# Down phase and S5 parameters: loads placed later; RWKV norm: one Newton chain for two groups; ScalarE: table loaded at the start

## The chip, the cores and the metric

The kernel runs on one core of a Trainium2 chip. The metric is the device time of one execution in microseconds, here the median of three runs. Two kernels are compared by such medians.

## The reference, cut to what matters

One layer of a decoder trunk on 1024 tokens of width 1024, in float32: three mixers (RWKV-7, a complex diagonal state space called S5, gated linear attention), each behind a sigmoid gate, then cross attention to 256 memory tokens, then a gated MLP with a short convolution, then a last RMSNorm.

```python
def rwkv7_mix(...):                       # 8 heads of 64, state S per head
    ...
    _, y = lax.scan(step, S0, seq)
    mean = jnp.mean(y, axis=-1, keepdims=True)
    var = jnp.mean(jnp.square(y - mean), axis=-1, keepdims=True)
    y = ((y - mean) * lax.rsqrt(var + RWKV_GN_EPS)).reshape(B, L, MIX_W) * ln_w + ln_b
    bonus = jnp.sum(r_h * k_h * r_k, axis=-1, keepdims=True) * v_h
    return (y + bonus.reshape(B, L, MIX_W)) * g

def conv_ffn(h, w_up, conv_w, conv_b, w_down):
    u = h @ w_up                          # 1024 x 5632, then a causal conv of width 3
    ...
    return (jax.nn.silu(gate) * val) @ w_down

    # the layer
    h = rms_norm(x, norm_mix)
    x = x + (gated sum of the three mixers) @ w_out
    x = x + cross_attention(rms_norm(x, norm_xattn), mem_n, ...)
    x = x + conv_ffn(rms_norm(x, norm_ffn), ...)
    return rms_norm(x, norm_final)
```

## The kernel before, in words

Every large product is made of three: a float32 operand is split into a high part, cast on ScalarE (ACT), and a low part, the difference, made on VectorE (DVE); high times high, high times low and low times high are added in PSUM (`split`, `mm3`, L111 to L115 and L127 to L132). Weights come by SyncE's DMA queue (SP) into a ring of four `wraw` tiles, are split into `whi` and `wlo`, and go to TensorE (PE). A scheduler writes a fixed instruction order for each engine from the order of the program, from priorities and from when it takes data to be there. An engine runs its list strictly in that order: an instruction that waits holds up all behind it, also on SP and on GpSimd (POOL), which issue the DMAs. SP's DMAs count on eight semaphores in turn, so each also waits until the DMA eight places ahead of it has landed.

**Start** (`start`, L228). SP loads S5's parameters `s5pk` (128x1076, issued in `run`, L1527), then vectors, the transposed memory `memT` and the first weights of the attention keys (`kv_k`). ACT scales `memT` into `mT` (L260); that is its first instruction with a function table. Then come four x tiles (`xt`), whose squares ACT sums (L212), and the weights of the next `kv_k` block.

**RWKV's second part** (`rw2`, L875). For each of 4 head pairs `pr` and 4 groups `g` of four chunks: products `vl`, `w`, `x`, `z`, `qm` (`rw2_prods`; DVE copies `ps_w` into `qw` at L963 before PE can do `z`), then four state steps one after the other (`rw2_steps`; the new state `s` is made half on DVE, half on ACT), then the norm of a group that was done before (`rw2_norm`, L1006): two reductions on DVE with a subtraction between, a square on ACT, `rsqrt_small` (three instructions, then three Newton rounds of three, L188 to L194) on 64x8 values, a scaling (L1021), four transposes, then scale and bias on ACT, plus the bonus (`ybo`, loaded by SP into a single buffer, L1012), times the gate product (`ps_g`), and a store by POOL. Between these, `fill` puts branch products (`ps_fm`) of the other mixers, which need nothing of RWKV.

**MLP and down phase** (`ffn`, `ffn_down` L1379). The MLP's 22 blocks end with `finish`, which writes the activations `c` to DRAM `d_act` by POOL (L1291), four writes a block, the last two adding to what is there; `c` and `u` live in the tiles `x0` to `x7` (even blocks `x0` to `x3`, odd ones `x4` to `x7`). The down product is done as seven products of halves, `a11`, `s1`, `s2`, `s4`, `s3`, `a12`, `a22`, each of 11 units; a unit reads one 128x512 tile of `d_act` (`araw`, L1410, four buffers), splits it, prepares one weight tile and does 12 matmuls. The weight quarters b11, b12, b22, b21 are loaded by SP (L1405) into places that the MLP leaves free. After the first product the residual x comes back from `d_x` into the same tiles `x0` to `x7` (L1472, POOL), and the sums are added to it (L1442). The `a11` units run between the last matmuls of the MLP.

## Time and profile before

| | before |
|---|---|
| median of three runs | 2205.38 us (2204.23 to 2213.23) |
| profiled execution, its own time | 2206.67 us |
| its span in the profile | 2204.9 us |
| PE busy | 2115.6 us, 96% |
| DVE busy | 1437.3 us, 65% |
| ACT busy | 956.8 us, 43% |
| DMA | 287.68 MB, mean 130 GB/s |

PE is busy 96% of the span, so about 89 us are left in which it does nothing; they lie in a few places, which the timeline of PE with its idle times shows one by one. A row of the timeline gives the start, the duration, the engine, line and operation, and in brackets how long the engine was idle before it and what ended that. The profiled execution is 1.29 us above the median of the runs, and 1.77 us of it lie around the span.

### The profile page before, as it was taken

The numbers are of one execution on the slowest core, as the hardware profiler recorded it, in microseconds if no ns is written. First come the engines' busy times: TensorE is split into PE (matmuls) and PEld (weight loads), VectorE is DVE, ScalarE is ACT, GpSimd is POOL, SyncE is SP. The second block draws the span as 40 slices with busy tenths as digits, with TensorE's granted clock in tenths as the row PEclk, the third lists the DMA queues.
The fourth block names the chain that finished last, engine by engine and source line by source line (L and its number), as shares of the span: only waits on it lengthen the run. The fifth ranks groups of instructions, "written<-read, shape, count | busy, mean of one in ns | idle before, by whom it ended". The sixth has DMA issues, their size and how long they took to land.

```text
span 2204.9 us, 29783 instructions
## 1 busy us (share of the span) xinstructions
PE 2115.6 (96%) x10686; PEld 1734.8 (79%) x10686; DVE 1437.3 (65%) x2813; ACT 956.8 (43%) x1692; POOL 201.6 (9%) x302
## 2 busy tenths in 40 slices
PE   7999999999999999999899999999999999988998
PEld 7877779878888887877787788777677777776886
DVE  6883743555657764676776655657677777777756
ACT  6423253554544442232334444555444444453452
POOL 0100000001111131002100000000011111111000
PEclk9999999999999999999999999999999999999999
DMA  8443332112343356565654232233566566597332
GB/s 259 141 115 91 104 107 55 33 55 63 115 129 121 124 187 179 155 169 129 171 183 142 85 103 79 84 119 108 127 157 167 154 127 135 118 280 248 100 95 105
DMA packets 314611, 287.68 MB, mean 130 GB/s; under 512 B 87408, under 2 KB 248864, under 8 KB 314464
## 3 DMA queue, kind: packets, MB, share of 16 engines
q1 hardware_dynamic: 285808, 203.98, 32.2%
q0 software_dynamic: 28656, 81.80, 13.4%
q8 instruction: 84, 1.38, 0.3%
q14 instruction: 63, 0.52, 0.1%
HBM read 191.38 MB, written 94.34 MB: 130 GB/s over the span
## 4 chain that ended last, share of the span: by engine, by line
PE 78%; DVE 8%; DMA 6%; ACT 4%; issue 2%; SPq 0%; DVEq 0%; ACTq 0%; POOLq 0%
PE ps_fm L132 11%; PE ps_fm L130 11%; PE ps_fm L131 11%; PE ps_q L1267 4%; PE ps_q L1268 4%; PE ps_dm L1438 4%; PE ps_q L1269 4%; PE ps_dn L1438 4%; PE ps_tm L130 3%; PE ps_tm L132 3%; PE ps_tm L131 3%; DMA a<-in_ffn_w_down 2%; PE ps_g L834 1%; DMA araw<-d_act 1%; ACT whi L114 1%
## 5 line engine op out<-in xcount | busy, mean ns | idle before, releaser
L115 DVE TENSOR_TENSOR wlo<-wraw,whi 128x512 fp32r<-128x512 f32 x320 | 220.4, 691 | 277.6 <-ACT whi L114 271.0
L114 ACT CAST whi<-wraw 128x512 fp32r<-128x512 f32 x320 | 197.7, 621 | 448.1 <-PE ps_fm L131 285.8
L130 PE MATMUL ps_fm<-hT,whi 128*128 128x512 f32 x800 | 316.9, 396 | 0.0
L132 PE MATMUL ps_fm<-hT,wlo 128*128 128x512 f32 x800 | 316.3, 395 | 0.0
L131 PE MATMUL ps_fm<-hT,whi 128*128 128x512 f32 x800 | 315.5, 394 | 0.0
L132 PEld LDWEIGHTS ps_fm<-hT,wlo 128*128 128x128 f32 x800 | 150.5, 188 | 33.4 <-issue 1.2
L131 PEld LDWEIGHTS ps_fm<-hT,whi 128*128 128x128 f32 x800 | 150.7, 188 | 32.7 <-issue 0.7
L130 PEld LDWEIGHTS ps_fm<-hT,whi 128*128 128x128 f32 x800 | 150.6, 188 | 31.9 <-issue 0.4
L1267 PE MATMUL ps_q<-a,whi 128*128 128x512 f32 x320 | 127.3, 398 | 6.7 <-ACT u L1345 5.2
L1268 PE MATMUL ps_q<-a,whi 128*128 128x512 f32 x320 | 126.1, 394 | 0.0
L1269 PE MATMUL ps_q<-a,wlo 128*128 128x512 f32 x320 | 126.0, 395 | 0.0
L1282 DVE SCALAR_TENSOR_TENSOR c<-u,cvn,c 128x1023 f32<-128x1023 f32 x80 | 102.5, 1284 | 19.3 <-ACT c L1279 18.0
L1438 PE MATMUL ps_dn<-whi,b 128*128 128x512 f32 x312 | 100.0, 399 | 8.5 <-ACT whi L114 8.5
L1291 POOL DMA_DIRECT2D d_act<-c x77 | 65.6, 859 | 406.9 <-DVE c L1286 258.2
L132 PE MATMUL ps_tm<-whi,a 128*128 128x512 f32 x256 | 101.5, 397 | 0.0
L114 ACT CAST whi<-s 128x512 fp32r<-128x512 f32 x80 | 49.6, 620 | 112.2 <-PE ps_q L1268 81.9
L114 ACT CAST b<-araw 128x512 fp32r<-128x512 f32 x72 | 44.7, 620 | 105.5 <-PE ps_dm L1438 37.8
L115 DVE TENSOR_TENSOR b<-araw,b 128x512 fp32r<-128x512 f32 x72 | 49.5, 690 | 60.9 <-ACT b L114 60.1
L1438 PE MATMUL ps_dm<-whi,b 128*128 128x512 f32 x264 | 82.9, 393 | 0.0
L115 DVE TENSOR_TENSOR wlo<-s,whi 128x512 fp32r<-128x512 f32 x80 | 55.0, 688 | 39.3 <-ACT whi L114 37.4
L130 PE MATMUL ps_fm<-a,whi 128*128 128x512 f32 x192 | 78.9, 411 | 1.7 <-ACT whi L114 1.6
L130 PE MATMUL ps_fm<-b,whi 128*128 128x512 f32 x192 | 76.5, 399 | 2.7 <-DVE c L1282 2.3
(537 smaller groups left out, 5066.3 us busy)
## 6 DMA issues: line engine op xcount, KB each, us to landing
wraw<-in_w_in SPq DMA_DIRECT2D x104, 256.0 KB, 3.0
araw<-d_act SPq DMA_DIRECT2D x77, 256.0 KB, 2.7
d_act<-c POOLq DMA_DIRECT2D x22, 768.0 KB, 7.5
d_gate<-gate SPq DMA_DIRECT2D x24, 512.0 KB, 3.0
gsg<-d_gate SPq DMA_DIRECT2D x24, 512.0 KB, 4.6
wraw<-in_ffn_w_up SPq DMA_DIRECT2D x48, 256.0 KB, 3.8
d_act<-c POOLq DMA_DIRECT2D x11, 1024.0 KB, 6.1
d_act<-c POOLq DMA_DIRECT2D x44, 256.0 KB, 5.3
```

What stands on the lines that cost most here:

```text
L114: self.nc.scalar.copy(hi, src)
L115: self.nc.vector.tensor_tensor(lo, src, hi.bitcast(F32), op=ALU.subtract)
L130: nc.tensor.matmul(ps, lh, rh, start=first, stop=False)
L131: nc.tensor.matmul(ps, lh, rl, start=False, stop=False)
L132: nc.tensor.matmul(ps, ll, rh, start=False, stop=last)
L834: nc.tensor.matmul(ps[:, j * 128:j * 128 + 128], BD[i][:, ci, :], AR[:, :, ci * 64:ci * 64 + 64], start=True, stop=True)
L1267: nc.tensor.matmul(ps, hi[:, s], t[0][:], start=first and k == 0, stop=False, skip_group_check=True)
L1268: nc.tensor.matmul(ps, hi[:, s], t[1][:], start=False, stop=False, skip_group_check=True)
L1269: nc.tensor.matmul(ps, lo[:, s], t[0][:], start=False, stop=last and k == 3, skip_group_check=True)
L1282: v.scalar_tensor_tensor(c[:, t:t1], src[:, t - d:t1 - d], cw(2 - d), c[:, t:t1], op0=ALU.mult, op1=ALU.add)
L1291: to = lambda n0, n1, h, **kw: nc.gpsimd.dma_start(st(n0, n1), src[h].to_broadcast([128, n1 - n0, 512]), **kw)
L1438: nc.tensor.matmul(o, a[x][:, s], w[y], start=first and k == 0, stop=last and k == 2, skip_group_check=True)
```

## The change

It has four parts. S5's parameters are loaded after the first four x tiles instead of first of all (`then` in `start`). ACT gets a multiplication of one column, with nothing to wait for but a memset, so that its function table is loaded then. In `rw2_norm` an even group g stops after the sums of squares; the odd group that follows makes one `rsqrt_small` on 64x16 for both and finishes both, one behind the other; `y` has three buffers for it. In `ffn_down` b12 is loaded during `s1` and b22 during `s2` (each was loaded one product earlier), and x comes by SP in halves of 512 columns, four after each of the products a11, s1, s2 and s4, the gains `gf` last; POOL has no loads left there.

```diff
--- before.py
+++ after.py
@@ -225,8 +225,12 @@
             if whole:
                 nc.scalar.mul(whole(k), ps[:, :n], g)
 
-    def start(self, pool):
-
+    def start(self, pool, then):
+
+
+        warm = self.cp.tile([128, 1], F32, name="warm")
+        self.nc.vector.memset(warm[:], 0.0)
+        self.nc.scalar.mul(warm[:], warm[:], 1.0)
         self.hT = self.new_T(pool, "hT")
         with ExitStack() as c2:
             p = self.pool(c2, "nrm")
@@ -270,6 +274,7 @@
                 norm(xs[h * 4:h * 4 + 4], "nmix", lambda k, l: self.hT[k, l][:, h * 512:h * 512 + 512])
             self.kv_k(0, us)
             load_x()
+            then()
             self.kv_k(1)
             self.kv_k(2)
             self.kv_k(3)
@@ -895,7 +900,7 @@
         f3 = lambda ap: ap.rearrange("p (c t) -> p c t", t=64)
         c3 = lambda ap: ap.rearrange("p (c k) -> p c k", c=4)
         n = 0
-        todo, prev = [], []
+        todo, prev, held = [], [], []
 
         def step():
             pr, g, ops = todo.pop(0)
@@ -904,7 +909,7 @@
 
         def norm():
             if len(prev) > 1:
-                self.rw2_norm(p, *prev.pop(0))
+                self.rw2_norm(p, held, *prev.pop(0))
         for hf in range(2):
             for pr in range(4):
                 t = ring[n % 2]
@@ -939,7 +944,7 @@
                     fill()
         step()
         norm()
-        self.rw2_norm(p, *prev.pop(0))
+        self.rw2_norm(p, held, *prev.pop(0))
 
     def rw2_prods(self, p, c0, t, R, c3):
 
@@ -999,36 +1004,45 @@
                 sn = S0[pr, (ci + 1) % 2]
                 v.tensor_scalar(sn[0:64, 0:64], o[64:128, 0:64], self.rw_pc[64:128, pr, 0, ci + 1:ci + 2], None, op0=ALU.mult)
                 nc.scalar.mul(sn[64:128, 64:128], o[64:128, 64:128], self.rw_pc[64:128, pr, 1, ci + 1:ci + 2])
-        y = p.tile([64, 8, 64], F32, tag="ysb", name="ysb", bufs=2)
+        y = p.tile([64, 8, 64], F32, tag="ysb", name="ysb", bufs=3)
         nc.scalar.copy(y[:], ps[0:64, :].rearrange("p (k f) -> p k f", k=8))
         return y
 
-    def rw2_norm(self, p, pr, g, y):
+    def rw2_norm(self, p, held, pr, g, y):
+
 
         nc, v = self.nc, self.nc.vector
-        ts = slice(g * 256, g * 256 + 256)
-        fs = slice(pr * 128, pr * 128 + 128)
-        bo = p.tile([128, 256], F32, tag="ybo", name="ybo", bufs=1)
-        nc.sync.dma_start(bo[:], self.d_bon[fs, ts])
-        m = p.tile([64, 2, 8], F32, tag="ym", name="ym", bufs=2)
         bc = lambda a: a.unsqueeze(2).to_broadcast([64, 8, 64])
-        v.tensor_reduce(m[:, 0], y[:], axis=AX, op=ALU.add)
-        v.scalar_tensor_tensor(y[:], bc(m[:, 0]), -1.0 / 64, y[:], op0=ALU.mult, op1=ALU.add)
+        if g % 2 == 0:
+            held.append(p.tile([64, 2, 16], F32, tag="ym", name="ym", bufs=2))
+        m, q = held[0], slice(g % 2 * 8, g % 2 * 8 + 8)
+        v.tensor_reduce(m[:, 0, q], y[:], axis=AX, op=ALU.add)
+        v.scalar_tensor_tensor(y[:], bc(m[:, 0, q]), -1.0 / 64, y[:], op0=ALU.mult, op1=ALU.add)
         sq = p.tile([64, 8, 64], F32, tag="ysq", name="ysq", bufs=1)
         nc.scalar.activation(sq[:], y[:], AF.Square)
-        v.tensor_reduce(m[:, 1], sq[:], axis=AX, op=ALU.add)
-        rs = self.rsqrt_small(p, m[:, 1], 1 / 64, 64e-5, 2, 8, 64)
-        v.tensor_tensor(y[:], y[:], bc(rs[:]), op=ALU.mult)
-        ps = self.psm.tile([128, 512], F32, tag="m", name="ps_yt")
-        for c in range(4):
-            nc.tensor.transpose(ps[:, c * 64:c * 64 + 64], y[:, 2 * c:2 * c + 2, :].rearrange("p h f -> p (h f)"), self.ident[0:64, 0:64])
-        yf = p.tile([128, 256], F32, tag="yf", name="yf", bufs=2)
-        nc.scalar.activation(yf[:], ps[:, 0:256], AF.Identity, bias=self.v("lnb", pr), scale=self.v("lnw", pr))
-        v.tensor_tensor(yf[:], yf[:], bo[:], op=ALU.add)
-        ps = self.psm.tile([128, 512], F32, tag="m", name="ps_g2")
-        nc.tensor.matmul(ps[:, 0:256], self.rw_gup[:, fs], self.rw_g[:, ts], start=True, stop=True)
-        v.tensor_tensor(yf[:], yf[:], ps[:, 0:256], op=ALU.mult)
-        nc.gpsimd.dma_start(self.yrw[fs, ts], yf[:])
+        v.tensor_reduce(m[:, 1, q], sq[:], axis=AX, op=ALU.add)
+        held.append((g, y))
+        if g % 2 == 0:
+            return
+        held.pop(0)
+        rs = self.rsqrt_small(p, m[:, 1], 1 / 64, 64e-5, 2, 16, 64)
+        fs = slice(pr * 128, pr * 128 + 128)
+        for q in range(2):
+            g, y = held.pop(0)
+            ts = slice(g * 256, g * 256 + 256)
+            bo = p.tile([128, 256], F32, tag="ybo", name="ybo", bufs=1)
+            nc.sync.dma_start(bo[:], self.d_bon[fs, ts])
+            v.tensor_tensor(y[:], y[:], bc(rs[:, q * 8:q * 8 + 8]), op=ALU.mult)
+            ps = self.psm.tile([128, 512], F32, tag="m", name="ps_yt")
+            for c in range(4):
+                nc.tensor.transpose(ps[:, c * 64:c * 64 + 64], y[:, 2 * c:2 * c + 2, :].rearrange("p h f -> p (h f)"), self.ident[0:64, 0:64])
+            yf = p.tile([128, 256], F32, tag="yf", name="yf", bufs=2)
+            nc.scalar.activation(yf[:], ps[:, 0:256], AF.Identity, bias=self.v("lnb", pr), scale=self.v("lnw", pr))
+            v.tensor_tensor(yf[:], yf[:], bo[:], op=ALU.add)
+            ps = self.psm.tile([128, 512], F32, tag="m", name="ps_g2")
+            nc.tensor.matmul(ps[:, 0:256], self.rw_gup[:, fs], self.rw_g[:, ts], start=True, stop=True)
+            v.tensor_tensor(yf[:], yf[:], ps[:, 0:256], op=ALU.mult)
+            nc.gpsimd.dma_start(self.yrw[fs, ts], yf[:])
 
 
     def gate_w(self, i, j):
@@ -1466,22 +1480,30 @@
                     a, w = act(an, b, ring()), weight(wn, b)
                     for i in range(4):
                         mm(o[i], a, w, i, first and b == 0, last and b == NB - 1)
-            product("a11", "b11", bank["A"], True, False, (load_w("b11"), load_w("b12")))
-            for tt in range(8):
-                x[tt] = self.xt(tt, f"x{tt}")
-                nc.gpsimd.dma_start(x[tt][:], self.d_x[tt * 128:tt * 128 + 128, :])
-            for q in range(2):
-                nc.gpsimd.dma_start(gf[q][:], A["norm_final"][q * 512:q * 512 + 512].partition_broadcast(128))
+            product("a11", "b11", bank["A"], True, False, (load_w("b11"),))
+
+            def load_x(t0, q):
+                for tt in range(t0, t0 + 4):
+                    if x[tt] is None:
+                        x[tt] = self.xt(tt, f"x{tt}")
+                    s = slice(q * 512, q * 512 + 512)
+                    nc.sync.dma_start(x[tt][:, s], self.d_x[tt * 128:tt * 128 + 128, s])
+            load_x(0, 0)
             for i in range(4):
                 add(i, 0, bank["A"][i], ALU.add)
             bank["B"] = second()
-            product("s1", "n1", bank["B"], True, False, (load_w("b22"),))
+            product("s1", "n1", bank["B"], True, False, (load_w("b12"),))
+            load_x(4, 1)
             for i in range(4):
                 add(4 + i, 1, bank["B"][i], ALU.subtract)
-            product("s2", "t2", bank["A"], False, False)
+            product("s2", "t2", bank["A"], False, False, (load_w("b22"),))
+            load_x(0, 1)
             for i in range(4):
                 add(i, 1, bank["A"][i], ALU.add)
             product("s4", "b22", bank["B"], False, True, (load_w("b21"),))
+            load_x(4, 0)
+            for q in range(2):
+                nc.sync.dma_start(gf[q][:], A["norm_final"][q * 512:q * 512 + 512].partition_broadcast(128))
             for i in range(4):
                 add(i, 1, bank["B"][i], ALU.add, True)
             product("s3", "t3", bank["A"], False, False)
@@ -1524,8 +1546,7 @@
         self.d_v = self.dr.tile([256, D], F32, name="d_v")
         hT, c1 = self.pool(left, "hT"), ExitStack()
         pk = self.pool(c1, "s5k").tile([128, 1076], F32, name="s5pk")
-        nc.sync.dma_start(pk[:], A["s5_par"])
-        self.start(hT)
+        self.start(hT, lambda: nc.sync.dma_start(pk[:], A["s5_par"]))
         todo = gates[:13]
 
         def fill(n):
```

The order on three engines. **First, SP at the start of the program**; `vc` are vectors, `wraw` weights of the keys. Before:

```order
L1527 DMA s5pk<-in_s_par 128x1076
L96 DMA vc<-in_cols 128x81
L254 DMA memT_131<-in_memT 128x2x256
L123 DMA wraw<-in_xa_wkv 128x4x128
L254 DMA memT_132<-in_memT 128x2x256
L123 DMA wraw<-in_xa_wkv 128x4x128
L254 DMA memT_133<-in_memT 128x2x256
L254 DMA memT_134<-in_memT 128x2x256
L123 DMA wraw<-in_xa_wkv 128x4x128 x2
L236 DMA xt<-in_x 128x1024 x4
L123 DMA wraw<-in_xa_wkv 128x4x128 x4
```

Now:

```order
L96 DMA vc<-in_cols 128x81
L258 DMA memT_133<-in_memT 128x2x256
L123 DMA wraw<-in_xa_wkv 128x4x128
L258 DMA memT_134<-in_memT 128x2x256
L123 DMA wraw<-in_xa_wkv 128x4x128
L258 DMA memT_135<-in_memT 128x2x256
L258 DMA memT_136<-in_memT 128x2x256
L123 DMA wraw<-in_xa_wkv 128x4x128 x2
L240 DMA xt<-in_x 128x1024 x4
L1549 DMA s5pk<-in_s_par 128x1076
L123 DMA wraw<-in_xa_wkv 128x4x128 x4
```

`s5pk` moved from the front to behind the four x tiles, still ahead of the second set of weights.

**Second, DVE in RWKV's second part**, from the end of one group's steps to the copy `qw` that PE waits for at 996 us; `ym` and `ysb` are the norm's sums and values, `rs_` is `rsqrt_small`, `gsg` belongs to a branch product. Before:

```order
L1000 TENSOR_SCALAR s_3_0_7901<-ps_p,rw_pc 64x64
L1015 TENSOR_REDUCE ym<-ysb 64x8
L1016 SCALAR_TENSOR_TENSOR ysb<-ym,ysb 64x512
L1019 TENSOR_REDUCE ym<-ysq 64x8
L188 TENSOR_SCALAR rs_x<-ym 64x8
L189 TENSOR_SCALAR rs_i<-rs_x 64x8
L1072 TENSOR_TENSOR gsg<-gsg,ps_fm 128x512 x2
L190 TENSOR_SCALAR rs_y<-rs_i 64x8
L192 TENSOR_TENSOR rs_b<-rs_y 64x8
L193 SCALAR_TENSOR_TENSOR rs_b<-rs_x,rs_b 64x8
L963 COPY qw_9099<-ps_w_9094 128x512
```

Now:

```order
L1041 TENSOR_TENSOR yf<-yf,ybo 128x256
L1005 TENSOR_SCALAR s_3_1_7906<-ps_p,rw_pc 64x64
L1044 TENSOR_TENSOR yf<-yf,ps_g_8962 128x256
L1005 TENSOR_SCALAR s_3_0_7904<-ps_p,rw_pc 64x64
L1041 TENSOR_TENSOR yf<-yf,ybo 128x256
L1044 TENSOR_TENSOR yf<-yf,ps_g_8977 128x256
L1019 TENSOR_REDUCE ym<-ysb 64x8
L1020 SCALAR_TENSOR_TENSOR ysb<-ym,ysb 64x512
L1023 TENSOR_REDUCE ym<-ysq 64x8
L1086 TENSOR_TENSOR gsg<-gsg,ps_fm 128x512 x2
L968 COPY qw_9051<-ps_w_9046 128x512
```

The five `rs_` instructions ahead of `qw` are gone; the ends of two groups' norms (`yf`, twice) stand one behind the other instead.

**Third, POOL and SP where the MLP ends.** `c_17285` is the activation of the last but one block, `c_17386` of the last; `x_17701` is tile `x2`, in which `c_17285` lies. POOL before:

```order
L1472 DMA x_17703<-d_x 128x1024
L1291 DMA d_act<-c_17285 128x3x512
L1472 DMA x_17701<-d_x 128x1024
L1472 DMA x_17707<-d_x 128x1024
L1472 DMA x_17705<-d_x 128x1024
L1474 DMA gf_17404<-in_norm_final 128x512
L1291 DMA d_act<-c_17386 128x512 x3
```

SP now, where `x_17546` is the same tile `x2` and the `a_` are weight tiles:

```order
L1419 DMA a_17806<-in_ffn_w_down 128x512
L1490 DMA x_17546<-d_x 128x512
L1419 DMA a_17843<-in_ffn_w_down 128x512
L1419 DMA a_17868<-in_ffn_w_down 128x512
L1419 DMA a_17893<-in_ffn_w_down 128x512
L1419 DMA a_17918<-in_ffn_w_down 128x512
L1490 DMA x_17833<-d_x 128x512
L1419 DMA a_17943<-in_ffn_w_down 128x512
```

The load of `x2`, which must wait for the writes of `c_17285`, moved from POOL's list into SP's, among the weight loads.

## Rows read from the trace of the kernel before

**Rows 1.** Page, part 1: busy time, share of the span and instructions of each engine.
```profile
PE 2115.6 (96%) x10686; PEld 1734.8 (79%) x10686; DVE 1437.3 (65%) x2813; ACT 956.8 (43%) x1692; POOL 201.6 (9%) x302
```
**Rows 2.** Timeline of the start: start, duration, engine, operation, idle time before and releaser.
```profile
0.81 0.39 SPq L1527 DMA_DIRECT2D s5pk<-in_s_par  x1
...
6.62 1.28 ACT L260 ACT_TABLE_LOAD   x1 [6.62 <-DMA memT<-in_memT]
...
19.75 2.30 ACT L114 CAST whi<-wraw 128x512 fp32r<-128x512 f32 x4
...
20.41 0.39 PE L130 MATMUL ps_fm<-mT,whi 128*128 128x256 f32 x1 [2.47 <-ACT whi L114]
```
**Rows 3.** DMA issues at 10.0 us: queue, count, size, us from issue to landing.
```profile
wraw<-in_xa_wkv SPq DMA_DIRECT2D x1, 256.0 KB, 8.5
```
**Rows 4.** Timeline of PE in RWKV's second part: products that waited.
```profile
980.51 0.46 PE L952 MATMUL ps_z<-qw,qvl 128*128 128x128 f32 x2 [1.59 <-DVE rs_b L193]
...
995.98 0.46 PE L952 MATMUL ps_z<-qw,qvl 128*128 128x128 f32 x2 [1.93 <-DVE rs_y L194]
...
1035.24 0.46 PE L952 MATMUL ps_z<-qw,qvl 128*128 128x128 f32 x2 [1.96 <-DVE rs_b L192]
...
1099.38 0.46 PE L952 MATMUL ps_z<-qw,qvl 128*128 128x128 f32 x2 [3.01 <-DVE rs_b L193]
```
**Rows 5.** Groups on DVE, 880 to 1155 us: count, busy us, mean ns, idle before.
```profile
L192 DVE TENSOR_TENSOR rs_b<-rs_y 64x8 f32<-64x8 f32 x48 | 10.3, 215 | 1.3
...
L193 DVE SCALAR_TENSOR_TENSOR rs_b<-rs_x,rs_b 64x8 f32<-64x8 f32 x48 | 9.6, 201 | 1.4
L194 DVE SCALAR_TENSOR_TENSOR rs_y<-rs_b,rs_y 64x8 f32<-64x8 f32 x48 | 8.2, 171 | 1.3
```
**Rows 6.** Stretches of 10 us: busy times by engine, PE's granted clock, DMA share, GB/s.
```profile
990.00:1000.00 10.00, 7.53 (x51) 6.81 (x51) 8.38 (x20) 2.72 (x5) 2.48 (x2) 0.87 0.42 142
1000.00:1010.00 10.00, 10.00 (x47) 8.54 (x47) 3.94 (x8) 3.38 (x7) 0.00 (x0) 0.79 0.25 53
```
**Rows 7.** Line L1012, the loads of `ybo`, last line of the answer.
```profile
DMA to landing us min/median/max: 2.2/2.3/6.5
```
**Rows 8.** Timeline of PE at the MLP's end and into the down phase.
```profile
1956.51 0.78 PE L1267 MATMUL ps_q<-a,whi 128*128 128x512 f32 x1 [3.90 <-ACT u L1345]
...
2005.63 0.79 PE L1438 MATMUL ps_dn<-whi,b 128*128 128x512 f32 x1 [8.47 <-ACT whi L114]
...
2011.49 0.39 PE L1438 MATMUL ps_dm<-whi,b 128*128 128x512 f32 x1
```
**Rows 9.** Timeline of ACT at the same place.
```profile
2003.09 0.62 ACT L114 CAST b<-araw 128x512 fp32r<-128x512 f32 x1 [16.31 <-DMA araw<-d_act]
2004.43 0.62 ACT L114 CAST b<-araw 128x512 fp32r<-128x512 f32 x1 [0.73 <-DMA araw<-d_act]
```
**Rows 10.** Timeline of SP at the same place.
```profile
1973.49 14.96 SPq L1405 DMA_DIRECT2D a<-in_ffn_w_down  x17
1989.35 0.33 SPq L1410 DMA_DIRECT2D araw<-d_act  x1
```
**Rows 11.** DMA issues at 1989.2 us: size and us to landing.
```profile
araw<-d_act SPq DMA_DIRECT2D x1, 256.0 KB, 13.7
```
**Rows 12.** Timeline of POOL at the same place.
```profile
1971.66 1.26 POOL L1291 DMA_DIRECT2D d_act<-c  x1 [6.15 <-DMA d_act<-c]
1984.10 1.65 POOL L1472 DMA_DIRECT2D x<-d_x  x3 [11.17 <-DVE b L1427]
```
**Rows 13.** DMA queues, 1989 to 1992 us: packets, MB, share of the 16 engines' time.
```profile
q0 software_dynamic: 217, 0.78, 66.1%
q1 hardware_dynamic: 223, 0.42, 37.0%
```
**Rows 14.** The same, 1977 to 1980 us.
```profile
q0 software_dynamic: 197, 0.40, 72.4%
```
**Rows 15.** Page, part 6: DMA issues by line: size, median us to landing.
```profile
d_act<-c POOLq DMA_DIRECT2D x22, 768.0 KB, 7.5
```

## The prediction

> **What bounds the kernel now.** I read the page's table of busy times first: PE is busy for 2115.6 of 2204.9 us [rows 1]. A change that leaves PE's work as it is can gain only from the 89 us in which PE stands, and the views that count are PE's timeline with the idle time before each product, and behind it the timeline of the engine that ended that idle time. The instruction order differs from the one before in three stages only: the start, RWKV's second part (880 to 1155 us) and the end of the MLP. PE's idle times there are the whole stake. At the start PE waits 2.47 us for a cast of weights [rows 2]. In RWKV's second part four products `ps_z` wait 1.59, 1.93, 1.96 and 3.01 us for DVE, which is in a Newton round at that moment [rows 4]. Where the MLP ends, PE stands for 8.47 us until 2005.63, and its matmuls then last 0.79 us until 2011.49, when they are back at 0.39 [rows 8]. I call this place the seam.
>
> **The start.** Two edits lie here. The table load of 1.28 us stands in front of ACT's first scaling and begins when `memT` lands at 6.62 [rows 2]; loaded earlier, it is off that path. `s5pk`, 128x1076 floats or 0.55 MB, no longer goes ahead of `memT` [rows 2]; at the 0.40 MB/us that the queues move together elsewhere [rows 13], that is 1.4 us, and with its issue some 2 us. Together they let PE begin about 3.5 us sooner. But PE then runs into its next wait sooner. The products at 20.41 need weights of the second key block [rows 2]; their load is issued at 10.0 and takes 8.5 us, so it lands near 18.7 [rows 3]; ACT casts it 1 us later, behind the squares [rows 2]. Ahead of these weights lie the same bytes as before, since `s5pk` moved behind the x tiles and not behind the weights. Thus the 3.5 us are given back in a longer idle time at that place. What is left is that ACT gets its x tiles sooner and has finished the squares when the weights land: cast at 18.8 instead of 19.75. I take **-0.9 us**, with -1.05 (cast at the landing) and +0.5 (`s5pk` keeps the queue from the weights for a third of its time) as ends. The added memset and multiplication run before any data has landed, and cost nothing.
>
> **RWKV's norm.** A chain has three Newton rounds of 215 + 201 + 171 ns [rows 5], 1.76 us, and three instructions ahead of them at about the same price, 0.5 us. Eight of sixteen chains go, 8 x 2.3 = 18.4 us of DVE; The eight that stay have twice the elements (64x16 for 64x8), a shape that no row shows: at worst they take twice as long and DVE saves nothing; by the nearest row, ACT's cast of 512 columns in 0.62 us [rows 9], eight columns more are 0.01 us, and I take that. But DVE is no bound here; only what stands ahead of a `qw` counts. The four waits are 1.59 + 1.93 + 1.96 + 3.01 = 8.49 us [rows 4]. The order shows that at the first three the `rs_` instructions ahead of `qw` are gone: I count 5.0 of their 5.48 us. At the fourth ten go, but two `yf` instructions come ahead of it: 1.0 us. PE's granted clock was 0.87 and then 0.79 in the two stretches from 990 us [rows 6]; against full speed that is (0.13 + 0.21) x 10 = 3.4 us, and as three waits stand near it, I give back half, 1.7 us. What is new is a burst: after an odd group's sums the ends of two norms follow each other, and in some places an `ym` or two `yf` come ahead of a `qw` that had none. No row shows this cover; three such places at 0.7 us make 2.2 us. The sum is -5.0 - 1.0 - 1.7 + 2.2 = **-5.5 us**. The ends are 0 (every burst costs what a chain cost) and -10.2 (all waits and half the clock gone). The load of `ybo` keeps its single buffer; it mostly lands after 2.3 us [rows 7], beside the next `qw` and state steps.
>
> **The seam.** PE waits for ACT's `whi` [rows 8], but ACT had stood 16.31 us for an `araw` until 2003.09 and then 0.73 for the next [rows 9]: two tiles of `s1` stand in ACT's list ahead of the cast of the last `a11` unit. SP issued the first of these reads at 1989.35, behind seventeen weight loads that took it 14.96 us [rows 10], and it took 13.7 us to land [rows 11], where the same 256 KB took 8.5 at the start [rows 3]. So the bytes in front of it are the cause. From 1989 to 1992 us POOL's queue q0 moved 0.78 MB and took 66.1% of the engines' time, SP's q1 0.42 MB with 37.0% [rows 13]: 1.20 MB in 3 us, 0.40 MB/us. POOL's part is seven of the eight x tiles and `gf`, 7 x 0.52 + 0.52 = 4.2 MB. They now come by SP, most of them much later, and b12 and b22 come a product later.
>
> By volume alone 4.2 / 0.40 = 10.5 us go, the read lands at about 1992.5, and no stall is left. But SP's list has a new wait. The load of x2 stands there among weight loads, in place of POOL's, and must wait until block 20's activations have left that tile. On POOL the three x loads behind that were held 11.17 us until 1984.10; the trace names DVE's `b`, which had long been done, and the last write, which adds to `d_act`, had been issued at 1971.66 [rows 12], so it took about 12.4 us. The median of such writes is 7.5 us [rows 15], and with q0 free of x it may be shorter: x2 can go between 1979 and 1984, and I take 1980, nearer the median. Until then SP, with all that stands behind x2, waits: fifteen loads and then the read, 16 x 0.262 = 4.2 MB. Beside them go the writes of block 21, of which the adding ones are dear: q0 needed 72.4% of the engines for 0.40 MB in 3 us [rows 14], so twice the share per MB of [rows 13]; I count them as 2.6 MB. From 1980 on that is 6.8 / 0.40 = 17 us, and 1.7 for the last to land: 1998.7, the second read about 2000, against 2003.1 and 2004.4. PE resumes some 4 us sooner. A cast of a later `araw` moves ahead of ACT's `u` near 1956 (PE waits 3.90 there [rows 8]) and may cost 0.5 to 1.2 us, but as long as a stall remains at the seam, that stall takes it in. Later, x6's half waits on block 21's writes the same way, about 2000, while PE needs the reads behind it only after 2016. I take **-4 us**; the ends are +1 (nothing gained, ACT's moved cast paid) and -10.8, worked out below.
>
> **Rivals.** *The seam's wait goes wholly.* If block 20's adding write lands in half the time since q0 carries no x beside it, SP never stands, and the volume counts alone. Then 8.47 us go, and of the slow matmuls behind (1.0 to 0.5 of full speed over 5.86 us [rows 8], 2.9 us) all, less 1.0 for ACT's moved cast: -10.4 to -10.8. With the start and the norm: -0.9 - 5.5 - 10.4 = -16.8. For it speaks that q0 took two thirds of the engines [rows 13]; against it the slow adding writes [rows 14], which stay. The Trainium skill, "DMA: Bandwidth & Descriptors", section "Queues, rings and completion order", says that each DMA engine takes turns, packet by packet, among the queues that have work. By that rule, weight loads alone would have every turn, and this rival would be the likelier; the shares of 66.1 and 37.0% fit turns between two busy queues, but no row here shows SP's queue alone.
>
> *The waits only change places.* SP stands at x2 until 1984, as POOL did, and from there 17 + 1.7 us end at 2002.7, where the read landed before; in RWKV's part the bursts eat half. -0.9 + 0 - 2.5 = -3.4 us. For it speaks that the 11.17 us of POOL's wait [rows 12] are measured beside this very list.
>
> *Slower: `ybo`.* Its single buffer makes the second group's load start only after the first group's add, one behind the other, where a whole group's time lay between before. If it lands in 6.5 us, as it did at worst [rows 7], instead of 2.3, DVE stands some 4 us in each of eight pairs, and half of that hits a `qw`: 16 us, against the 5 us that start and seam bring: +11, about 2217. The median speaks against it; it decides from a landing of some 4 us on, where it eats the norm's gain.
>
> **How the numbers follow.** The sum is -0.9 - 5.5 - 4 = -10.4 us: the profiled execution's 2206.67 would become 2196.3. It lay 1.29 us above the median of 2205.38, so the forecast for the median is **2195.0 us**. The first rival gives 2188.6, the second 2202.0, the third about 2217. I give the forecast 0.45, the rivals 0.22, 0.25 and 0.08. A measurement of this kernel tells a change from none at about 0.5%, or 11.0 us: faster is below 2194.4, slower above 2216.4. The forecast lies at that bound, so it gives slightly under half of its chance to faster (0.20), and with the first rival's 0.22 that is 0.42; slower takes 0.07, most of the third; the rest, 0.51, is within 0.5%. For 8 in 10 the range goes from 2186 (first rival with the norm's best end partly reached) to 2203 (second rival and a microsecond).
>
> **What would show it.** The start: PE's first product some 3.5 us earlier, a longer idle time ahead of the second key block, and the cast there near 18.8. The norm: `rs_b` at 64x16 with 24 in each line, no idle time left at the first three `ps_z`, and DVE without waits for `ybo`. The seam: no x on POOL, SP idle at the load of x2 until about 1980, `araw` landing near 1999, and PE idle for about 4 us there. I am wrong if the seam's idle time is gone or as long as before, or if new waits of over 1 us each line up at `qw` in RWKV's part.

## The result and the profile after

| | before | after |
|---|---|---|
| median | 2207.45 us (6 runs, 2204.23 to 2213.23) | 2196.35 us (6 runs, 2191.79 to 2199.34) |
| ratio | | 0.9947, 95% interval 0.9936 to 0.9957 |
| profiled execution, its own time | 2206.67 us | 2197.81 us |

The changed kernel takes 11.1 us less by the medians; the ratio, 0.53% below 1, has an interval that leaves out no change. Of three runs of before, the median had been 2205.38. The page's part 1 of the changed kernel, which answers to [rows 1]:

```profile
PE 2115.0 (96%) x10686; PEld 1733.7 (79%) x10686; DVE 1420.6 (65%) x2718; ACT 958.6 (44%) x1693; POOL 196.6 (9%) x292
```

PE does the same work, and its busy time in all is the same to 0.6 us; of the 8.8 us by which the span is shorter (2204.9 to 2196.1), 8.2 are idle time. Within a stage busy time changes too, with the granted clock. Both traces hold all 10,686 products, so the n-th of one can be set against the n-th of the other (in RWKV's part some change places): where its start is earlier by more than the start of the one ahead, time was won there. Below, "ahead" means the median of that difference over the products of a stretch. The changed kernel's products are 0.7 us behind before at 85 to 170 us, 9.1 us ahead at 1155 to 1250 us, 6.8 us ahead at 1990 us, and 9.3 us ahead from 2030 us on.

**The start.** Timeline of ACT and PE in the changed kernel, against [rows 2]:

```profile
4.31 0.91 ACT L264 ACTIVATE mT<-memT,vc 128x256 fp32r<-128x256 f32 x2 [1.77 <-DMA memT<-in_memT]
...
18.76 0.62 ACT L114 CAST whi<-wraw 128x512 fp32r<-128x512 f32 x1 [1.13 <-DMA wraw<-in_xa_wkv]
...
38.90 1.06 ACT L212 ACTIVATE sq<-xt 128x1024 f32<-128x1024 f32 x1 [4.75 <-DMA xt<-in_mem]
```
```profile
5.78 0.58 PE L130 MATMUL ps_fm<-mT,whi 128*128 128x256 f32 x1 [5.78 <-ACT whi L114]
...
19.43 0.39 PE L130 MATMUL ps_fm<-mT,whi 128*128 128x256 f32 x1 [3.02 <-ACT whi L114]
```

PE's first product and the squares of the memory tiles in the kernel before:

```profile
8.99 0.58 PE L130 MATMUL ps_fm<-mT,whi 128*128 128x256 f32 x1 [8.99 <-ACT whi L114]
```
```profile
38.66 1.06 ACT L212 ACTIVATE sq<-xt 128x1024 f32<-128x1024 f32 x1 [1.87 <-DMA xt<-in_mem]
```

PE begins 3.2 us sooner, the cast of the second key block comes at 18.76, and PE goes on there 0.98 us sooner than before. But the next thing that comes by DMA, the squares of the memory tiles, starts at 38.90; before it was 38.66. There the microsecond is lost again. From 8 to 40 us SP's queue takes 91 to 108% of the engines' time in every 8 us, in both kernels, so in that time the queue has no room to bring anything sooner.

**RWKV's second part.** The four products `ps_z` of [rows 4], in the order of the program; the first and the last still wait, the others have no idle time in front:

```profile
976.52 0.35 PE L957 MATMUL ps_z<-qw,qvl 128*128 128x128 f32 x1 [0.33 <-DVE qw L968]
...
992.82 0.35 PE L957 MATMUL ps_z<-qw,qvl 128*128 128x128 f32 x1
...
1026.83 0.35 PE L957 MATMUL ps_z<-qw,qvl 128*128 128x128 f32 x1
...
1090.45 0.35 PE L957 MATMUL ps_z<-qw,qvl 128*128 128x128 f32 x1 [0.41 <-DVE qw L968]
```

Four of the larger waits that came in their place, in the same timeline:

```profile
979.42 0.38 PE L999 MATMUL ps_p<-qx,qz 128*128 128x128 f32 x1 [1.10 <-ACT s L1006]
...
1056.85 0.35 PE L957 MATMUL ps_x<-wv,wak 128*128 128x128 f32 x1 [1.79 <-DMA wv<-rw_tm]
...
1072.67 0.35 PE L957 MATMUL ps_z<-qw,qvl 128*128 128x128 f32 x1 [1.16 <-DVE qw L968]
...
1088.92 0.35 PE L957 MATMUL ps_x<-wv,wak 128*128 128x128 f32 x1 [1.38 <-DMA wv<-rw_tm]
```

Two of the four wait for loads of the next pair's data and one for ACT's half of the state `s`; only one is at a `qw`. The granted clock in the two stretches of [rows 6] and around 1100 us (busy times by engine, clock, DMA share, GB/s), first after, then before:

```profile
990.00:1000.00 10.00, 9.89 (x72) 8.76 (x71) 5.21 (x10) 3.41 (x8) 2.50 (x2) 1.00 0.80 250
1000.00:1010.00 10.00, 10.00 (x59) 8.73 (x58) 8.26 (x22) 3.25 (x6) 2.51 (x2) 1.00 0.55 134
...
1095.00:1105.00 10.00, 9.34 (x53) 7.87 (x54) 7.85 (x12) 4.93 (x10) 0.00 (x0) 1.00 0.90 297
```
```profile
1095.00:1105.00 10.00, 6.99 (x38) 5.96 (x37) 6.87 (x21) 4.16 (x9) 0.00 (x0) 0.83 0.75 228
```

The clock no longer leaves 2.4 GHz here. Before, it fell to 1.2 GHz for a part of these stretches, each time right behind a wait at `ps_z` (1.93 us at 995.98, 3.01 us at 1099.38). But the changed kernel has a fall of its own just ahead of them, from 868.0 to 871.4 us, where before has none. The stretches there, first after, then before:

```profile
860.00:870.00 10.00, 8.18 (x53) 7.43 (x52) 4.01 (x7) 5.30 (x9) 0.00 (x0) 0.90 0.56 189
870.00:880.00 10.00, 9.74 (x66) 8.62 (x65) 7.11 (x13) 4.90 (x10) 0.00 (x0) 0.93 0.69 189
```
```profile
860.00:870.00 10.00, 8.18 (x64) 7.56 (x64) 5.43 (x9) 6.14 (x11) 0.00 (x0) 1.00 0.56 190
870.00:880.00 10.00, 8.31 (x53) 6.73 (x52) 5.89 (x12) 4.16 (x9) 0.00 (x0) 1.00 0.77 185
```

On DVE a Newton instruction of 64x16 lasts 195 to 209 ns, and there are 24 of each instead of 48 (against [rows 5]):

```profile
L192 DVE TENSOR_TENSOR rs_b<-rs_y 64x16 f32<-64x16 f32 x24 | 5.0, 209 | 0.8
...
L193 DVE SCALAR_TENSOR_TENSOR rs_b<-rs_x,rs_b 64x16 f32<-64x16 f32 x24 | 4.7, 195 | 0.7
```

No instruction waited for `ybo`; the line's last row, against [rows 7]:

```profile
DMA to landing us min/median/max: 2.3/2.5/5.6
```

**The seam.** Timelines of SP, POOL, ACT and PE, against [rows 8 to 12]; then PE's and the DMA engines' stretches of 3 us:

```profile
1955.03 7.59 SPq L1419 DMA_DIRECT2D a<-in_ffn_w_down  x9
1973.44 0.33 SPq L1490 DMA_DIRECT2D x<-d_x  x1
...
1985.69 0.33 SPq L1424 DMA_DIRECT2D araw<-d_act  x1
...
1987.07 1.68 SPq L1424 DMA_DIRECT2D araw<-d_act  x3
```
```profile
1963.73 1.28 POOL L1305 DMA_DIRECT2D d_act<-c  x1 [7.02 <-DMA d_act<-c]
...
1984.85 1.28 POOL L1305 DMA_DIRECT2D d_act<-c  x1 [8.33 <-DMA d_act<-c]
```
```profile
1993.08 0.62 ACT L114 CAST b<-araw 128x512 fp32r<-128x512 f32 x1 [13.11 <-DMA araw<-d_act]
1996.22 0.62 ACT L114 CAST b<-araw 128x512 fp32r<-128x512 f32 x1 [2.52 <-DMA araw<-d_act]
```
```profile
1997.41 0.79 PE L1452 MATMUL ps_dn<-whi,b 128*128 128x512 f32 x1 [7.06 <-ACT whi L114]
```
```profile
1968.00:1971.00 3.00, 3.00 (x14) 2.44 (x13) 3.00 (x4) 1.35 (x4) 0.00 (x0) 1.00 0.95 173
1971.00:1974.00 3.00, 3.00 (x14) 2.44 (x14) 2.89 (x4) 2.35 (x4) 0.00 (x0) 1.00 0.06 12
```

SP issues nothing from 1962.6 to 1973.44. It stands at the load of x2 until the adding write that POOL issued at 1963.73 has landed; from 1971 to 1974 the DMA engines are busy 6% of the time. The first read of `s1` is cast at 1993.08, the second 3.1 us later, and PE is idle for 7.06 us in place of 8.47.

### The profile page after: what moved, and what is told of

The parts are those of the page before. It is cut to its first block, busy times and chain, and to the rows that moved or that the text cites. A ratio compares the mean times of both kernels' runs of the same rounds, so it can differ in the third digit from the quotient of the medians.

```text
span 2196.1 us, 29686 instructions
## 1 busy us (share of the span) xinstructions
PE 2115.0 (96%) x10686; PEld 1733.7 (79%) x10686; DVE 1420.6 (65%) x2718; ACT 958.6 (44%) x1693; POOL 196.6 (9%) x292
## 4 chain that ended last, share of the span: by engine, by line
PE 50%; DVE 4%; DMA 3%; ACT 2%; issue 1%; DVEq 0%; SPq 0%; ACTq 0%; POOLq 0%
PE ps_dn L1452 5%; PE ps_q L1281 5%; PE ps_q L1282 5%; PE ps_q L1283 4%; PE ps_dm L1452 4%; PE ps_fm L130 3%; PE ps_fm L132 3%; PE ps_fm L131 3%; PE ps_tm L130 2%; PE ps_tm L132 2%; PE ps_tm L131 2%; PE ps L1281 1%; ACT whi L114 1%; DMA araw<-d_act 1%; PE ps_p L999 1%
## 5 line engine op out<-in xcount | busy, mean ns | idle before, releaser
L1281 PEld LDWEIGHTS ps_q<-a,whi 128*128 128x128 f32 x320 | 61.0, 191 | 24.2 <-ACT u L1359 5.6
```

Source lines behind the costliest of these rows:

```text
L1281: nc.tensor.matmul(ps, hi[:, s], t[0][:], start=first and k == 0, stop=False, skip_group_check=True)
```

## The experiments

The three parts alone came first, each added to the kernel before, and with them a version that moves only SP's wait. Kernels are told from one another in two ways: by their median against the kernel before, measured beside them, and by the products' position in the trace. The second tells the stages apart, where a median of the whole can't.

**The start alone.**

```
 start(...): warm tile, memset, scalar.mul; then() behind the first load_x()
 run():      self.start(hT, lambda: nc.sync.dma_start(pk[:], A["s5_par"]))
 (rw2_norm and ffn_down as before)
```

> The kernel before with the start's part alone (s5pk behind the first four x tiles, ACT's table loaded first). Theory: the start is bound by the bytes in front of the weights and of the memory tiles, so what PE gains ahead of 20 us (3.2 us at its first product) is lost again by 80 us, where the whole change stood 0.7 us behind the kernel before; the time is within 2 us of the kernel before, more likely above than below. If the prediction's -0.9 us holds, PE stands about 0.9 us ahead at 80 us and to the end. The products of RWKV's second part must then wait as before, four times at ps_z for Newton rounds, and the seam must show 8 to 9 us of idle PE.

Measured: 2208.33 us against 2207.53, ratio 1.0006 (0.9996 to 1.0015), so +0.8 us with an interval of -0.9 to +3.3. PE was 3.1 us ahead at its first product, 1.3 at the second key block, and 0.8 behind at 85 to 170 us. No gain is left.

**The norm alone.**

```
 rw2, rw2_steps, rw2_norm as in the change; start, run and ffn_down as before
```

> The kernel before with RWKV's norm in pairs alone. Theory: this part carries the change: PE wins 4.7 us of waits between 880 and 1155 us and, since the granted clock then doesn't fall near 1000 and 1100 us, 5.1 us more, 9.8 in all; time 2197 to 2199. Rival: the clock's part is luck of one execution; then the granted clock falls in this stretch as before, and the gain is 4 to 6 us, time 2202 to 2204. Rival: the clock fell at the start of the changed kernel's stretch because of the start's part; then 868 us shows full clock here.

Measured: 2199.20 us, ratio 0.9964 (0.9950 to 0.9977), -8.3 us. From 860 to 1200 us PE wins 9.3 us. The stretches of the clock:

```profile
990.00:1000.00 10.00, 9.89 (x72) 8.77 (x71) 5.06 (x10) 3.33 (x7) 2.49 (x2) 1.00 0.85 260
1000.00:1010.00 10.00, 10.00 (x59) 8.70 (x58) 8.07 (x23) 3.31 (x6) 2.52 (x2) 1.00 0.49 124
...
1095.00:1105.00 10.00, 10.00 (x56) 8.11 (x56) 7.74 (x13) 4.87 (x10) 0.00 (x0) 1.00 0.87 291
```

The clock stays up in these stretches with the norm's part alone, so what keeps it up is neither the start's part nor one execution, and at 868 us it doesn't fall here either. At the seam this kernel loses 1.9 us against before: PE comes there 10 us sooner and idles 10.26 us, before 8.47.

**The down phase alone.**

```
 ffn_down as in the change; all else as before
```

> The kernel before with the down phase's part alone. Theory: SP stands at the load of x2 until block 20's adding write has landed, 9 to 11 us in which the DMA engines have little to do, the reads of s1 land 3 to 4 us sooner than before, the second of them late because of block 21's adding write; PE's idle time at the seam goes from 8.5 to about 7 us, and the stretch at half clock behind it gets shorter: 2 to 3 us in all, time 2204 to 2206. The prediction had 4 us: 2203.5.

Measured: 2203.18 us, ratio 0.9982 (0.9973 to 0.9991), -4.4 us, about what the prediction had and more than I expected of this run. PE idles 2.65 us at the seam, where I expected 7. SP stands at x2 here too, from 1971.4 to 1980.49, and the reads come from 1998.1 on, 5 us later than in the changed kernel; but PE also reaches the seam later, by 8.8 us, since RWKV's part was as slow as before.

**SP's wait moved to POOL.** This is the one that tells what was left at the seam.

```diff
-                    nc.sync.dma_start(x[tt][:, s], self.d_x[...])
+                    eng = nc.gpsimd if (tt, q) in ((2, 0), (6, 1)) else nc.sync
+                    eng.dma_start(x[tt][:, s], self.d_x[...])
```

> The changed kernel, where the halves of x2 and x6 that must wait for d_act's writes are loaded by POOL, all others by SP as in the change. Theory (SP's wait is what is left of the seam's stall): SP never stands for 9 us, the weight loads behind go out at once while the DMA engines had been idle, the reads of s1 land before PE needs them, and the idle time of 7.06 us and the half clock behind it go: 6 to 9 us less than the changed kernel, 2187.5 to 2190.5. Rival (volume and the adding writes): the same bytes stand before the reads and block 21's adding write still slows them; the idle time stays over 5 us and the time within 2.5 us of 2196.35.

Measured: 2189.89 us, ratio 0.9921 (0.9908 to 0.9934), 6.5 us less than the changed kernel. POOL, ACT, and the stretches:

```profile
1977.21 0.60 POOL L1491 DMA_DIRECT2D x<-d_x  x1 [11.39 <-DMA d_act<-c]
```
```profile
1988.04 0.62 ACT L114 CAST b<-araw 128x512 fp32r<-128x512 f32 x1 [6.79 <-DMA araw<-d_act]
1989.39 0.62 ACT L114 CAST b<-araw 128x512 fp32r<-128x512 f32 x1 [0.74 <-DMA araw<-d_act]
```
```profile
1971.00:1974.00 3.00, 3.00 (x15) 2.43 (x14) 3.00 (x5) 1.91 (x3) 0.00 (x0) 1.00 1.10 256
...
1986.00:1989.00 3.00, 3.00 (x15) 2.47 (x14) 0.31 (x1) 0.62 (x1) 1.28 (x1) 1.00 1.05 404
1989.00:1992.00 3.00, 3.00 (x14) 2.13 (x13) 3.00 (x6) 2.61 (x5) 0.00 (x0) 1.00 1.11 245
```

POOL now stands for 11.39 us at x2, where little is behind it; SP had stood for 10.8. The DMA engines work on from 1971 to 1974, the reads come 5 us sooner, and PE has no idle time at the seam and no half clock behind it: between 1990 and 2030 us it wins 10.4 us, where the change won 2.5.

**Two chains in the pair.** All of the regrouping stays, only the number of chains goes back.

```diff
-        rs = self.rsqrt_small(p, m[:, 1], 1 / 64, 64e-5, 2, 16, 64)
+        r8 = [self.rsqrt_small(p, m[:, 1, h * 8:h * 8 + 8], 1 / 64, 64e-5, 2, 8, 64) for h in range(2)]
...
-            ... bc(rs[:, q * 8:q * 8 + 8]) ...
+            ... bc(r8[q][:]) ...
```

> The changed kernel, where the odd group makes two Newton chains of 64x8, one for each group, in place of one of 64x16; all else of the pairs stays. Theory (the number of chains on DVE is what counts): between 880 and 1155 us most of the 9.3 to 9.8 us comes back, DVE is 17 to 18 us busier, products ps_z wait for Newton rounds again and the granted clock falls at least once in the stretch: 2201 to 2206. Rival (regrouping alone, the even group's chain no longer in front of its own successor, makes the gain): within 2 us of the changed kernel's 2196.35.

Measured: 2202.93 us, ratio 0.9982 (0.9973 to 0.9991). In RWKV's part nothing of the gain is left: PE loses 1.2 us there against before (the kernel with the down phase alone, whose norm is that of before, loses as much), where the changed kernel wins 9.8. Two products of the timeline, and the clock:

```profile
995.20 0.46 PE L957 MATMUL ps_z<-qw,qvl 128*128 128x128 f32 x2 [1.93 <-DVE rs_y L194]
1031.29 0.51 PE L957 MATMUL ps_z<-qw,qvl 128*128 128x128 f32 x2 [2.01 <-DVE rs_y L194]
```
```profile
1095.00:1105.00 10.00, 8.81 (x46) 7.74 (x47) 6.45 (x17) 4.74 (x11) 0.00 (x0) 0.83 1.10 300
```

The waits for Newton rounds and the falls of the clock are back together. What gains is the shorter list on DVE ahead of `qw`, not the order of the groups.

**All of x on POOL.** b12 and b22 stay a product later.

```diff
-                    nc.sync.dma_start(x[tt][:, s], self.d_x[...])
+                    nc.gpsimd.dma_start(x[tt][:, s], self.d_x[...])
```

> The changed kernel with all halves of x loaded by POOL; its list then has both halves of a tile one behind the other, as early as before the change, while b12 and b22 stay a product later. Theory (SP's wait at x2 is the price, and the bytes of x ahead of the reads matter less than those of b12): the seam's idle time is under 3 us, 2189 to 2193. Rival (the bytes matter): POOL's x takes half of the DMA engines' time as before, the reads of s1 land as late as in the changed kernel or later, idle time 6 to 9 us, 2195 to 2199.

Measured: 2197.73 us, ratio 0.9958 (0.9944 to 0.9972). My theory fell, the rival held. SP has no wait, but PE idles 7.83 us at the seam and wins only 0.6 us there against before:

```profile
1997.60 0.80 PE L1452 MATMUL ps_dn<-whi,b 128*128 128x512 f32 x1 [7.83 <-ACT whi L114]
```

The DMA queues from 1978 to 1981 us stand as in [rows 13]:

```profile
q1 hardware_dynamic: 226, 0.41, 37.8%
q0 software_dynamic: 227, 0.77, 67.0%
```

So the bytes of x on POOL are what held the reads before, and taking them away was worth some 10 us; SP's wait gave back about 8 of them. That b12 and b22 come a product later is worth little beside x on POOL, since this kernel has it too.

**The start again**, on the kernel with x2 and x6 on POOL: with s5pk still later, with the old start, and with s5pk late but no early table load.

```diff
             load_x()
-            then()
             self.kv_k(1)
...
             self.kv_v(0)
             norm_half(1)
+            then()
```

> The kernel with x2 and x6 on POOL (2189.89), and s5pk loaded behind the memory tiles and the first weights of the values, some 15 us later, but well before its first use near 84 us. Theory (the start is bound by the bytes ahead of the weights): now 0.55 MB are gone from in front of the second key block and of the memory tiles, 1.4 to 2 us at 0.3 to 0.4 MB/us; PE stands 0.5 to 1.5 us ahead of the kernel before at 90 us, in place of 0.8 to 0.95 us behind it: 2187.5 to 2188.7. Rival (squares, transposes and DVE's chains bind the start, not the bytes): nothing changes, 2189 to 2191.

Measured: 2186.86 us, ratio 0.9905 (0.9892 to 0.9919). PE is 2.4 us ahead of before at 85 to 170 us, more than the 0.5 to 1.5 expected.

> The kernel with x2 and x6 on POOL, and the start as in the kernel before (s5pk first, no early table load). Theory (the start's part loses 0.7 to 0.9 us): 2188.5 to 2189.5, PE at 90 us as in the kernel before, within 0.8 us. If the prediction's -0.9 us holds, it is 2190.8 or more.

Measured: 2190.44 us, ratio 0.9925 (0.9911 to 0.9938), 0.55 us from the kernel with the changed start; PE 0.2 us ahead. The two can't be told apart. From the kernel with s5pk late, 2186.86 us beside it, the medians part by 3.6 us, but their intervals overlap a little; it is PE's place in the trace, 2.4 us ahead against 0.2, that tells them apart.

```diff
-        warm = self.cp.tile([128, 1], F32, name="warm")
-        self.nc.vector.memset(warm[:], 0.0)
-        self.nc.scalar.mul(warm[:], warm[:], 1.0)
```

> The kernel with s5pk loaded late (2186.86), without the early table load on ACT: the 1.28 us stand again between the first memory tile and ACT's first scaling. Theory (the start is bound by the bytes ahead of the second key block): PE's first product comes 1.3 us later, its idle time before the second key block is that much shorter, and PE stands 1.9 to 2.6 us ahead of the kernel before at 90 us, as with the early load; 2186 to 2188. Rival (the table load carries the start's gain now that the bytes are gone): PE stands about 1.1 us ahead, 2188 to 2189.

> The same kernel as with s5pk loaded late, again, beside the one without the early table load: 2186 to 2188, PE 1.9 to 2.6 us ahead at 90 us if its place there is the kernel's and not the execution's; 1 us or less if it was chance.

Measured side by side: 2186.58 us without the early table load (ratio 0.9899, 0.9883 to 0.9915), 2186.46 with it (0.9895, 0.9879 to 0.9911). PE is 2.4 and 4.0 us ahead at 85 to 170 us. By the medians the table load is worth nothing in this kernel. Without it PE's first product comes 0.3 and 0.8 us later than in the two runs with it, not 1.3. The memory tiles' squares in the two runs with s5pk late:

```profile
36.18 1.06 ACT L212 ACTIVATE sq<-xt 128x1024 f32<-128x1024 f32 x1 [1.87 <-DMA xt<-in_mem]
```
```profile
35.34 1.06 ACT L212 ACTIVATE sq<-xt 128x1024 f32<-128x1024 f32 x1 [1.85 <-DMA xt<-in_mem]
```

They start 2.7 and 3.6 us sooner than in the changed kernel (38.90). This is the place that the change left as it was.

Where PE won time in each kernel, in us against before (products ahead at 85 to 170; from 850 to 866 on to 1155 to 1250; from 1985 to 1995 on to after 2030):

| kernel | start | RWKV's part | seam |
|---|---|---|---|
| changed | -0.7 | 9.8 | 2.5 |
| start alone | -0.8 | -0.7 | 0.0 |
| norm alone | -0.8 | 9.3 | -1.9 |
| down alone | 1.2 | -1.2 | 5.3 |
| two chains | 0.3 | -1.2 | 4.2 |
| all x on POOL | 0.5 | 9.9 | 0.6 |
| x2, x6 on POOL | -1.0 | 8.8 | 10.4 |
| the same, old start | 0.2 | 10.4 | 10.1 |
| the same, s5pk late | 2.4, 4.0 | 9.6, 7.9 | 10.9, 11.0 |
| the same, no table load | 2.4 | 11.1 | 10.5 |

Each figure is one execution's: where RWKV's part is that of before it still lies at -0.7 and -1.2, so differences of about a microsecond say nothing. One pattern is larger. Of kernels that differ in RWKV's gain alone, or in that and the start, the one with the gain wins less at the seam: -1.9 against 0 in before, 2.5 against 4.2 with two chains and 5.3 with the down phase alone. The parts don't simply add up.

## Why the prediction was right, and where its terms were off

The time was forecast at 2195.0 us and came at 2196.35; the forecast's gain of 10.4 us was measured as 11.1. The three parts alone sum to +0.8 - 8.3 - 4.4 = -11.9. That the median came 1.35 us from the forecast is partly luck: the norm's term was too small, the start's and (in the changed kernel) the seam's too large, and the errors nearly cancel. The mechanisms are those of the prediction, except for one step at the start and one at the seam.

**The start (-0.9 forecast; +0.8 measured, between -0.9 and +3.3).** The steps up to the second key block came as written: PE's first product 3.2 us sooner, longer idle time before the block, the cast at 18.76 (18.8 forecast). What failed is that I ended the sum there. The argument that took back the 3.5 us, the same bytes ahead of the next load, holds for the memory tiles at 38.9 us as well, and takes back the rest. The kernel with s5pk loaded late shows it from the other side. Of four kernels with the old start, before among them, the positions at 85 us lie between -0.8 and +1.2; of five with the new one between -1.0 and +0.5. By these positions, that s5pk moved is worth nothing at the place where the change put it, and 2.4 to 4.0 us behind the memory tiles.

**RWKV's norm (-5.5 forecast; -8.3 measured alone, where its trace wins 9.3 us and loses 1.9 at the seam; 9.8 us in the changed kernel's trace).** The mechanism holds: the chains ahead of `qw`, which the run with two chains shows directly. Two terms were mis-sized. The waits: I had -5.0 - 1.0 + 2.2 = -3.8 us; over the products of before's 880 to 1155 us PE's idle time fell from 15.95 to 11.27 us, so -4.7. The four `ps_z` lost 7.75 of their 8.49 us, the fourth 2.6 of its 3.01, where I had counted 1.0. Against that stand six new waits of over 0.8 us, 7.7 us in sum and not 2.2: one at a `qw` (1.16), three at ACT's half of `s`, two at the pair's loads; smaller waits elsewhere that went make up the rest. The clock: I gave back half of what two stretches had lost, 1.7 us. All of it went, and a third stretch that stood in no row, (1 - 0.83) x 10 = 1.7 us near 1100: 5.1 us in sum. The changed kernel gave 1.7 of that back, (0.10 + 0.07) x 10, with its fall at 868 us, behind a wait of 1.78 us that before has as well, without a fall. From 860 us on its idle time is 6.1 us less, so 6.1 + 5.1 - 1.7 = 9.5 of the 9.8 us of the trace. With the norm's part alone, which has no fall at 868, it is 4.6 + 5.1 = 9.7 for 9.3. That 64x16 takes as long as 64x8 held: 195 to 209 ns against 171 to 215.

**The seam (-4 forecast; -4.4 measured alone, 2.5 us in the changed kernel's trace).** SP's wait came as forecast. On before's timeline PE is here 6.8 us later than in the changed kernel, so x2's load at 1973.44 stands for 1980.2 (1980 forecast), the first read's cast at 1993.08 for 1999.9 (1998.7), the second's at 1996.22 for 2003.0 (2000). The step that failed is the last one: the second read lay 3.1 us behind the first, not 1.3, because block 21's adding write was issued at 1984.85, just ahead of both reads (1985.69 and 1987.07), and ran beside them. From 1989 to 1992 us POOL's queue has most of the engines' time:

```profile
q0 software_dynamic: 186, 0.38, 68.4%
```

I had let its bytes pass before them. Where both reads are issued ahead of that write, the second is cast 1.35 us (x2 and x6 on POOL) and 1.37 us (two chains) behind the first, as I had it. So PE idled for 7.06 us where I had about 4. The 1.7 us that the sum gives the last load to land stands in no row; x2's own 256 KB, loaded while the engines had little else to do, took 2.6 us from issue to landing. The wait near 1956, which I feared the moved cast would lengthen, is 4.49 us for 3.90, but another of 1.25 us at 1935 went, and from 1900 to 1990 us nothing was lost.

**The rivals.** *The seam's wait goes wholly* didn't happen in the changed kernel, but its price was right: with SP's wait taken away, the median is 2189.89 (2188.6 forecast), and the seam gives 10.4 us (10.4 to 10.8). Its condition, that the write lands in half the time, didn't come: the write took 9.7 us with q0 free of x. From 1986 to 1989 us the changed kernel's trace shows SP's queue alone:

```profile
q1 hardware_dynamic: 650, 1.18, 105.4%
```

It moved 1.18 MB in 3 us, where it had 0.42 beside POOL's; there the two had moved 223 and 217 packets [rows 13], nearly as many each. Both agree with the rule that I weighed in the prediction: the Trainium skill, "DMA: Bandwidth & Descriptors", section "Queues, rings and completion order", says that each DMA engine takes turns, packet by packet, among the queues that have work. But SP's queue moved nothing from 1968 to 1974 us, since the wait lies on the issuing engine, ahead of all queues. *The waits only change places* fits the seam halfway and RWKV's part not at all. *Slower: `ybo`* didn't come: its loads land in 2.5 us at the median, at most 5.6, and none was waited for.

**Still open.** Between 1250 and 1600 us the changed kernel loses 2.7 us against before, in stages that the change doesn't touch; every other kernel loses 0.1 to 2.6 us there too. The traces show where: PE idles 1.7 us more, and the clock falls twice, behind waits of 2.28 us at 1519.39 and 3.53 at 1570.80, where in before it fell once, behind 2.01 us at 1560.36. Why is open; before's profiled execution may just have been a good one there. Also open in part is why the seam gains 2.5 us in the changed kernel and 5.3 in the one with the down phase's part alone. There block 20's adding write was out of the way after 8.1 us, not 9.7, and block 21's was issued behind the first read (1993.55 after 1992.78), not ahead of it, so that the first read was cast 5.3 us after its issue, not 7.4. Why the first write was quicker no run tells.

## What to carry to other kernels

A load that must wait for a late write belongs on a queue with nothing urgent behind it: two tiles' halves moved from SP to POOL were worth 6.5 us, more than half of what the whole change had brought. When a transfer is moved to a later place, follow the sum past the first wait to the last one that needs the same bytes, since everything ahead of it only shifts the idle time. And where PE waits for a microsecond or two again and again, read the granted clock of every such stretch, as the clock can be worth as much as the waits.

## What the runs showed of the hardware

In RWKV's part the granted clock fell with the waits. In the traces of the four kernels with sixteen Newton chains it fell to 1.2 GHz two to four times between 880 and 1155 us. In the eight traces with eight chains it fell once in two (all x on POOL, near 1089 us; x2 and x6 on POOL, near 1091; both behind a wait at a pair's load) and in six not at all. With the norm's part alone the 5.1 us that this gave back are more than the 4.6 us of waits that went. In the changed kernel, which had a fall at 868 us instead, it is 3.4 against 6.1.

And the writes that add are dear: from 1968 to 1971 us in the changed kernel, with SP standing, POOL's queue alone needed 94.7% of the engines' time for 0.52 MB, where SP's queue alone moved 1.18 MB in as long a stretch. From 1977 to 1980 us, with the first of block 21's writes, which don't add, the same POOL queue needed 32.1% for 0.39 MB. That is some twice the time for a byte, and it points to the adding, not to the queue.

```profile
q0 software_dynamic: 265, 0.52, 94.7%
```
```profile
q0 software_dynamic: 112, 0.39, 32.1%
```

The write of 768 KB issued at 1963.73 took 9.7 us until the load behind it could go (8.1 with the down phase alone, 12.4 in before, 12.7 with x2 and x6 on POOL), and whichever engine had that load next in its list, POOL or SP, stood for it.
